# Decay rows of one head side by side in DRAM, so that their loads read runs of 4 KB

## The chip, the cores and the metric

One Trainium2 chip, and of it one core. The metric is the device time of one execution in microseconds (us). The shapes are fixed: one sequence of 1024 tokens with 16 learned meta tokens ahead of it, 1024 channels, 8 heads.

## The reference

One layer of a bidirectional encoder. Each token is normalised and projected once; from the projection come a Fourier branch, and a gated-DeltaNet branch with q, k, v and two sets of decay and beta logits. The delta rule runs forwards and backwards over chunks of 64 tokens. The part of it that the change touches:

```
g = cumsum(g within a chunk of 64)
diff = g[..., :, None] - g[..., None, :]
decay = where(lower, exp(where(lower, diff, 0)), 0)
a_mat = where(strict, (k_beta @ k^T) * decay, 0)
t_mat = inverse(I + a_mat)
qk    = where(lower, (q @ k^T) * decay, 0)
```

So every head, direction and chunk needs a 64 x 64 matrix of exponentials of differences of one row g: one g down the partitions, the same g along the free dimension. After the scan both branches are gated, merged and projected; a mixture of 64 experts (top group, top two experts in it) and a final norm follow.

## The kernel before

The work goes in stages. `norm1` normalises and transposes the input. `gates` computes all decay rows. `heads` makes q, k and v of the 8 heads; `meta` treats the 16 meta tokens. `middle` does the Fourier branch and the gate projections. Then come the scan over chunks (`scan`), the merge (`delta`), the output projection (`output`) and the experts, whose weights stream from DRAM. In `heads` there are 24 tiles (k, v and q of each head, in the order k0 v0 k1 q0 k2 v1 k3 q1 v2 q2 v3 q3, then the same for heads 4 to 7). For each, TensorE does 72 projection matmuls (`product`, L220) into the tile `proj`; ScalarE copies them out (`pad`, L356); VectorE does a convolution of 5 taps (`acc`, eight instructions on L373); ScalarE applies SiLU (`kraw`, `vraw`, `qT`).

For a k tile, `k_stage` transposes (L435), sums squares (L438), takes a reciprocal root in a chain of small VectorE and GpSimd steps (`rk_x` L98, `rk_y` L105, `rk_t` L106 to L108, `rk_y` L109), and scales on ScalarE (`ktok`, L446). `k_back` transposes back on TensorE (L456) to `kT`.

`decay` (L484) builds the 64 x 64 matrices of one head: tile `F`, 128 partitions x 1024 numbers, where a partition is a row in a chunk (two halves of 64), and the free dimension is 16 chunk pairs and directions (`v n`) x 64 columns (`c`). The row along the free dimension must reach all 64 partitions of a half; that is done by a load from the DRAM tensor `dF`, which `gates` wrote (L339). There are two loads for one F (L489), one for each half. Then VectorE subtracts (L494) and limits (L495), and ScalarE exponentiates (L496). `chunks` multiplies F with k k^T (L511, twice, stored to `dL` by L513) or with q k^T (L516, stored to `dQK` by L517). There are 16 such tiles, two for a head; `fp` holds two buffers, so a load of F waits until the store of the F two before it has landed.

`dF` is stored as transposed: its row n is one column of `G` or `FL`, and the 128 columns are ordered `(v n h)`, the head last:

```
L336  self.dF = self.dram("dF", [2, 128, 2, 64])
L339  nc.sync.dma_start(self.dF[i].rearrange("n a c -> n (a c)"), ts[...])
L488  src = self.dF[i].rearrange("(n h) a c -> n h a c", h=8)[:, h, half]
L489  nc.sync.dma_start(F[half]..., src.unsqueeze(0).to_broadcast([64, 16, 64]))
```

`inverse` (L521) gathers `dL` of four heads into `M`, eliminates on VectorE (L688, L690, pairs of growing and shrinking size, ending with the MEMSET on L692) and stores `dT` for the scan.

All loads named here are issued by SyncE (SP), one after the other, and each engine works through its own queue in a fixed order. A scheduler writes these orders when the program is built, from the code and its own estimates; a change in the shape of a transfer therefore moves other instructions too.

Of the kernel before, what the change touches and what calls it, by code (L numbers as in the profile page):

```python
# [8 lines left out]
F32 = mybir.dt.float32  # L9
# [103 lines left out]
class Kern:  # L113
# [116 lines left out]
    def gates(self, abT):  # L230
        tc, nc, io, cp = self.tc, self.nc, self.io, self.c1
# [4 lines left out]
        gp = self.gp  # L236
# [9 lines left out]
        for half in range(2):  # L246
            hs = slice(64 * half, 64 * half + 64)
            for v in range(2):
                d = 0 if half == v else 1
                src = pv[hs, :, 16 * d:16 * d + 16].rearrange("p n (k h) -> p k n h", k=2)  # L250
# [41 lines left out]
        G = cp.tile([128, 136], F32, name="G")  # L292
# [22 lines left out]
        FL = gp.tile([128, 136], F32, name="FL")  # L315
# [11 lines left out]
                    nc.vector.tensor_scalar(FL[hs, cs], G[hs, cs], -1.0, None, op0=OP.mult)  # L327
        self.G, self.PL = G, PL
        tps = self.pprep.tile([128, 512], F32, name="prep")
        nc.tensor.transpose(tps[:, 0:128], G[:, :128], self.ident)  # L330
        nc.tensor.transpose(tps[:, 128:256], FL[:, :128], self.ident)
        nc.tensor.transpose(tps[:8, 256:272], FL[:16, 128:136], self.ident[:16, :16])
        ts = gp.tile([128, 272], F32, name="ts")
        nc.scalar.activation(ts[:, :256], tps[:, :256], AF.Copy)
        nc.scalar.activation(ts[:8, 256:272], tps[:8, 256:272], AF.Copy)
        self.dF = self.dram("dF", [2, 128, 2, 64])  # L336
        self.dFm = self.dram("dFm", [8, 16])
        for i in range(2):
            nc.sync.dma_start(self.dF[i].rearrange("n a c -> n (a c)"), ts[:, 128 * i:128 * i + 128])  # L339
        nc.sync.dma_start(self.dFm, ts[:8, 256:272])  # L340


# [141 lines left out]
    def decay(self, h, d, i):  # L484
        nc = self.nc
        d["F"] = F = self.fp.tile([128, 2, 8, 64], F32, name="F")
        for half in range(2):
            src = self.dF[i].rearrange("(n h) a c -> n h a c", h=8)[:, h, half]  # L488
            nc.sync.dma_start(F[64 * half:64 * half + 64].rearrange("p v n c -> p (v n) c"),  # L489
                              src.unsqueeze(0).to_broadcast([64, 16, 64]))  # L490
        bc = [128, 2, 8, 64]
        c = (self.G, self.PL)[i][:, :128].rearrange("p (v n h) -> p v n h", v=2, h=8)[:, :, :, h:h + 1].to_broadcast(bc)
        m = (self.maskq, self.maskl)[i]
        nc.vector.tensor_tensor(F, *((F, c) if i == 0 else (c, F)), op=OP.subtract)  # L494
        nc.vector.tensor_tensor(F, F, m[:, :, None, :].to_broadcast(bc), op=OP.min)  # L495
        nc.scalar.activation(F, F, AF.Exp)  # L496
# [1284 lines left out]
```

## Time and profile before

| what | value |
|---|---|
| median of 3 runs | 1853.7 us (1852.88 to 1856.15) |
| profiled execution, its time | 1855.85 us |
| profiled execution, its span | 1854.0 us |
| mean granted clock of TensorE | 0.965 |
| TensorE busy | 1726.9 us, 93% of the span |
| VectorE busy | 1043.0 us, 56% |
| ScalarE busy | 696.6 us, 38% |
| GpSimd busy | 194.0 us, 10% |
| DMA packets | 149102, of which 68663 under 512 B |
| heads stage, about | 92 to 464 us |

The span is the profiled execution seen by the profiler; its time is 1.85 us longer, and lies 2.15 us above the median. Busy shares are means over stages with different limits. The stage of the heads is where the slices of the page show TensorE's busy share and its granted clock below full again and again.

### The profile page before, as it was taken

The page shows a single profiled execution, that of the slowest core. Times are in us where ns is not written, and L with a number is a line of the kernel's source. Part 1 is how long each engine was busy: PE and PEld are TensorE (multiplying, and loading weights), DVE is VectorE, ACT ScalarE, POOL GpSimd, SP SyncE. Part 2 cuts the span into 40 slices and gives each one's busy share as a digit, 9 for nine tenths or more (in the row PEclk, how much of TensorE's full clock was granted, in tenths as well). Part 3 has the DMA queues.
Part 4 walks back from the last instruction along what each step waited for, and adds up shares of the span by engine and source line. Part 5 has one row for each costly group of instructions (what it writes and reads, how often), then busy time and mean ns, then how long its engine had stood idle before and what let it go on. Part 6 is the DMA issues. An engine that isn't in the chain of part 4 may idle for free. (4 is left out here: it accounts for less than half of the span.)

```text
span 1854.0 us, 26490 instructions
## 1 busy us (share of the span) xinstructions
PE 1726.9 (93%) x10018; PEld 1237.6 (67%) x10018; DVE 1043.0 (56%) x2196; ACT 696.6 (38%) x1539; POOL 194.0 (10%) x300
## 2 busy tenths in 40 slices
PE   7968989978999999799999999999789999999996
PEld 6968988978978888466766677888634443434342
DVE  6646558777955898456566554641633444434433
ACT  5645546454432211444444443421233332323231
POOL 2000001000010001013323200000110111001100
PEclk9988999988999999899999999999989999999998
DMA  4143542334466346734434327735389999999995
GB/s 156 51 124 114 157 140 93 102 106 132 140 197 177 121 159 205 191 109 137 143 120 120 109 95 239 230 119 204 129 350 419 416 419 419 419 419 415 420 419 202
DMA packets 149102, 391.16 MB, mean 211 GB/s; under 512 B 68663, under 2 KB 70879, under 8 KB 123999
## 3 DMA queue, kind: packets, MB, share of 16 engines
q1 hardware_dynamic: 132744, 337.65, 49.7%
q0 software_dynamic: 14736, 51.02, 8.7%
q8 instruction: 81, 1.33, 0.3%
q10 hardware_dynamic: 1488, 0.73, 0.2%
q14 instruction: 53, 0.43, 0.1%
HBM read 328.28 MB, written 65.26 MB: 212 GB/s over the span
## 5 line engine op out<-in xcount | busy, mean ns | idle before, releaser
L220 PE MATMUL proj<-xh,wh 128*128 128x346 f32 (+5 forms) x1080 | 395.4, 366 | 16.9 <-ACT zt L1696 8.6
L220 PE MATMUL proj<-xl,wh 128*128 128x346 f32 (+4 forms) x1080 | 394.9, 366 | 0.0
L220 PE MATMUL proj<-xh,wl 128*128 128x346 f32 (+4 forms) x1080 | 393.7, 366 | 0.0
L220 PEld LDWEIGHTS proj<-xh,wh 128*128 128x128 f32 (+1 forms) x1080 | 207.8, 192 | 38.1 <-ACT zt L1696 9.4
L220 PEld LDWEIGHTS proj<-xl,wh 128*128 128x128 f32 (+1 forms) x1080 | 207.5, 192 | 18.7 <-issue 5.8
L220 PEld LDWEIGHTS proj<-xh,wl 128*128 128x128 f32 (+1 forms) x1080 | 207.0, 192 | 19.3 <-issue 6.7
L373 DVE SCALAR_TENSOR_TENSOR acc<-pad,convw,acc 128x520 f32<-128x520 f32 x192 | 136.1, 752 | 21.9 <-ACT acc L369 21.8
L860 ACT ACTIVATE wh<-wr 128x1024 fp32r<-128x1024 f32 (+2 forms) x77 | 77.2, 1004 | 130.8 <-PE proj L220 67.6
L861 DVE TENSOR_TENSOR wl<-wr,wh 128x1024 fp32r<-128x1024 f32 (+2 forms) x77 | 88.8, 1155 | 42.6 <-ACT wh L860 42.4
L1343 DVE SCALAR_TENSOR_TENSOR ea<-ea,gw,gu 128x256 f32<-128x256 f32 x32 | 15.4, 480 | 171.7 <-ACT ea L1342 171.7
L688 DVE TENSOR_TENSOR tmp<-M 128x62 f32<-128x62 f32 (+30 forms) x124 | 105.9, 854 | 7.1 <-DMA M<-dL 5.5
L690 DVE TENSOR_TENSOR M<-M,tmp 128x62 f32<-128x62 f32 (+30 forms) x124 | 105.9, 854 | 1.8
L741 DVE SCALAR_TENSOR_TENSOR R<-main,egn,svtok 128x128 f32<-128x128 f32 x128 | 44.8, 350 | 101.5 <-PE main L739 101.4
L750 ACT ACTIVATE vd<-main,vdec 128x128 f32<-128x128 f32 x128 | 46.9, 366 | 137.0 <-PE main L748 136.8
L758 DVE SCALAR_TENSOR_TENSOR S<-S,egl,dS 128x128 f32<-128x128 f32 x240 | 72.7, 343 | 39.6 <-PE dS L757 39.2
L739 PE MATMUL main<-S,skq 128*64 128x128 f32 x1024 | 86.1, 288 | 0.1
L1342 ACT ACTIVATE ea<-gu 128x256 f32<-128x256 f32 x32 | 12.3, 384 | 183.0 <-PE gu L1338 183.0
L1368 DVE TENSOR_TENSOR yl<-dn,yh 128x512 fp32r<-128x512 f32 x64 | 44.2, 690 | 59.9 <-ACT yh L1367 55.0
L739 PEld LDWEIGHTS main<-S,skq 128*64 128x64 f32 x1024 | 54.7, 137 | 31.0 <-DVE so L761 16.5
L1367 ACT ACTIVATE yh<-dn 128x512 fp32r<-128x512 f32 x64 | 38.1, 595 | 97.4 <-PE dn L1365 97.0
L1338 PE MATMUL gu<-ml,gx 128*64 128x512 f32 x288 | 70.8, 607 | 4.1 <-DMA ml<-in_w_gu_dram 4.1
L1338 PE MATMUL gu<-mh,gx 128*64 128x512 f32 x288 | 67.0, 593 | 1.9 <-DMA mh<-in_w_gu_dram 1.9
(432 smaller groups left out, 3160.9 us busy)
## 6 DMA issues: line engine op xcount, KB each, us to landing
mh<-in_w_gu_dram SPq DMA_DIRECT2D x36, 1024.0 KB, 19.9
ml<-in_w_gu_dram SPq DMA_DIRECT2D x36, 1024.0 KB, 21.1
wr<-in_w_t_dram SPq DMA_DIRECT2D x52, 512.0 KB, 4.1
wx<-in_w_gu_dram SPq DMA_DIRECT2D x20, 1024.0 KB, 19.1
mh<-in_w_dn_dram SPq DMA_DIRECT2D x20, 1024.0 KB, 20.9
ml<-in_w_dn_dram SPq DMA_DIRECT2D x18, 1024.0 KB, 19.9
yh<-in_w_gu_dram SPq DMA_DIRECT2D x16, 1024.0 KB, 16.4
yl<-in_w_gu_dram SPq DMA_DIRECT2D x16, 1024.0 KB, 16.5
```

Source lines behind the costliest of these rows:

```text
L220: nc.tensor.matmul(o, w[:, k, :n], x[:, k, a:b], start=(m == 0), stop=(m == 23))
L373: nc.vector.scalar_tensor_tensor(o, pad[:, a + j:a + j + NT // 2], w[:, j:j + 1], o, op0=OP.mult, op1=OP.add)
L688: nc.vector.tensor_tensor(tv, M[:, j + 1:, j:j + 1].to_broadcast([np_, m, j]), M[:, j:j + 1, :j].to_broadcast([np_, m, j]), op=OP.mult)
L690: nc.vector.tensor_tensor(M[:, j + 1:, :j], M[:, j + 1:, :j], tv, op=OP.add)
L739: nc.tensor.matmul(ps[hs[half], i], kv[:, i, 2 * (p % 4) + half], st[half], start=True, stop=True)
L741: nc.vector.scalar_tensor_tensor(R, ps[:, 0], self.egn[:, col:col + 1], d["vtok"][p // 4][:, p % 4], op0=OP.mult, op1=OP.add)
L750: nc.scalar.activation(vd, ps[:, 2], AF.Copy, scale=self.vdec[:, col:col + 1])
L758: nc.vector.scalar_tensor_tensor(st[half], st[half], self.egl[:, half, col:col + 1], dS, op0=OP.mult, op1=OP.add)
L860: self.nc.scalar.activation(hi, src, AF.Copy)
L861: self.nc.vector.tensor_tensor(lo, src, hi.bitcast(F32), op=OP.subtract)
L1338: nc.tensor.matmul(pg[self.HS[i]], d["x"][:, 4 * kk + k, c:c + 64], w[:, 4 * i + k], start=(kk == 0 and k == 0), stop=(kk == 1 and k == 3))
L1368: nc.vector.tensor_tensor(yl[:, cs], pd, yh[:, cs].bitcast(F32), op=OP.subtract)
```

## The change

`gates` reorders the columns of `G` and `FL` from `(n h)` to `(h n)` with two VectorE copies into a new tile `GF`, transposes that instead, and stores `dF` as `[2, 2, 128, 64]`: kind, half, row `(h n)`, column. The store takes four DMAs of 64 columns instead of two of 128. The 16 rows of one head and half are then one run of 16 x 64 x 4 B = 4096 B, and `decay` loads that run to each of 64 partitions instead of 16 pieces of 256 B. Values and consumers are the same.

```diff
         tps = self.pprep.tile([128, 512], F32, name="prep")
-        nc.tensor.transpose(tps[:, 0:128], G[:, :128], self.ident)
-        nc.tensor.transpose(tps[:, 128:256], FL[:, :128], self.ident)
+
+        GF = gp.tile([128, 2, 128], F32, name="GF")
+        for i, t in enumerate((G, FL)):
+            nc.vector.tensor_copy(GF[:, i].rearrange("p (h n) -> p h n", h=8), t[:, :128].rearrange("p (n h) -> p h n", h=8))
+            nc.tensor.transpose(tps[:, 128 * i:128 * i + 128], GF[:, i], self.ident)
...
-        self.dF = self.dram("dF", [2, 128, 2, 64])
+        self.dF = self.dram("dF", [2, 2, 128, 64])
...
         for i in range(2):
-            nc.sync.dma_start(self.dF[i].rearrange("n a c -> n (a c)"), ts[:, 128 * i:128 * i + 128])
+            for a in range(2):
+                nc.sync.dma_start(self.dF[i, a], ts[:, 128 * i + 64 * a:128 * i + 64 * a + 64])
...
         for half in range(2):
-            src = self.dF[i].rearrange("(n h) a c -> n h a c", h=8)[:, h, half]
-            nc.sync.dma_start(F[64 * half:64 * half + 64].rearrange("p v n c -> p (v n) c"),
-                              src.unsqueeze(0).to_broadcast([64, 16, 64]))
+            src = self.dF[i, half, 16 * h:16 * h + 16].rearrange("n c -> (n c)")
+            nc.sync.dma_start(F[64 * half:64 * half + 64].rearrange("p v n c -> p (v n c)"), src.partition_broadcast(64))
```

The order of the instructions moves with it. In the changed kernel the lines of `heads` and after have numbers higher by 4 up to `decay` (L373 becomes L377, the chain of L106 to L109 keeps its numbers), and by 3 from there (L494 becomes L497, L511 becomes L514, L861 becomes L864).

VectorE, between the multiplication that ends the use of the first F (k of head 0) and the subtraction that waits for the load into its buffer (q of head 0), before and after:

```order
L511 SCALAR_TENSOR_TENSOR F<-prep,F 128x512 x2
L495 TENSOR_TENSOR F<-F,cst 128x1024
L373 SCALAR_TENSOR_TENSOR acc<-pad,convw,acc 128x520
L861 TENSOR_TENSOR wl<-wr,wh 128x1024
L373 SCALAR_TENSOR_TENSOR acc<-pad,convw,acc 128x520 x2
L98 TENSOR_SCALAR rk_x<-ssk 128x9
L494 TENSOR_TENSOR F<-F,G 128x1024
```

```order
L514 SCALAR_TENSOR_TENSOR F<-prep,F 128x512 x2
L98 TENSOR_SCALAR rk_x<-ssk 128x9
L497 TENSOR_TENSOR F<-F,G 128x1024
L435 MEMSET ssk 128x1
L377 SCALAR_TENSOR_TENSOR acc<-pad,convw,acc 128x520 x2
```

The subtraction has moved up: of the six instructions that stood between, one is left.

VectorE, the root chain of head 0 (`rk_x` to `rk_y`) and the first subtraction (k of head 0), before and after:

```order
L98 TENSOR_SCALAR rk_x<-ssk 128x9
L431 MEMSET ssk 128x1
L106 TENSOR_TENSOR rk_t<-rk_y 128x9
L107 TENSOR_TENSOR rk_t<-rk_t,rk_x 128x9
L108 TENSOR_SCALAR rk_t<-rk_t 128x9
L109 TENSOR_TENSOR rk_y<-rk_y,rk_t 128x9
L447 TENSOR_SCALAR km<-prep,rk_y 16x128
L861 TENSOR_TENSOR wl<-wr,wh 128x1024
L373 SCALAR_TENSOR_TENSOR acc<-pad,convw,acc 128x520 x3
L494 TENSOR_TENSOR F<-PL,F 128x1024
```

```order
L106 TENSOR_TENSOR rk_t<-rk_y 128x9
L377 SCALAR_TENSOR_TENSOR acc<-pad,convw,acc 128x520
L497 TENSOR_TENSOR F<-PL,F 128x1024
L377 SCALAR_TENSOR_TENSOR acc<-pad,convw,acc 128x520
L107 TENSOR_TENSOR rk_t<-rk_t,rk_x 128x9
L497 TENSOR_TENSOR F<-PL,F 128x1024
L498 TENSOR_TENSOR F<-F,cst 128x1024
L108 TENSOR_SCALAR rk_t<-rk_t 128x9
L498 TENSOR_TENSOR F<-F,cst 128x1024
L864 TENSOR_TENSOR wl<-wr,wh 128x1024
L109 TENSOR_TENSOR rk_y<-rk_y,rk_t 128x9
```

The chain of head 0 stood ahead of every F; now the first two subtractions stand inside it.

SP, from the store of k of head 1 (`dL`) to the loads of F for heads 2 and 3, before and after:

```order
L513 DMA dL<-F 64x2x512 x2
L517 DMA dQK<-F 128x1024
L489 DMA F<-dF 64x16x64 x4
L448 DMA dk<-ktok 128x1024
L199 DMA wr<-in_w_t_dram 128x1024
```

```order
L516 DMA dL<-F 64x2x512 x2
L493 DMA F<-dF 64x1024 x2
L520 DMA dQK<-F 128x1024
L493 DMA F<-dF 64x1024 x2
L521 DMA dkq<-qT 128x1024
```

The first of the two loads no longer stands behind the store of q of head 0.

## Rows read from the trace of the kernel before

**Rows 1.** The page, its first line and busy time of TensorE: us, share of the span, instructions.

```profile
span 1854.0 us, 26490 instructions
```

**Rows 2.** Busy time in four stretches (us from the span's start): length, then busy us and instructions of PE, PEld, DVE, ACT and POOL, then the granted clock of TensorE, the DMA share and GB/s.

```profile
92.00:278.00 186.00, 152.25 (x1133) 148.00 (x1131) 103.26 (x159) 93.02 (x198) 7.59 (x23) 0.90 0.44 133
278.00:464.00 186.00, 163.93 (x1145) 158.61 (x1146) 141.78 (x198) 94.02 (x221) 12.25 (x22) 0.91 0.34 108
464.00:740.00 276.00, 274.48 (x1435) 229.14 (x1434) 209.66 (x302) 73.20 (x108) 13.32 (x22) 1.00 0.52 166
...
1340.00:1854.00 514.00, 482.56 (x2186) 202.14 (x2186) 210.35 (x425) 159.27 (x297) 51.39 (x53) 0.97 0.95 391
```

**Rows 3.** The waits of PE between 92 and 464 us, the longest entry: who waited <- for whom: us in total, times, longest us.

```profile
PE prep L456 <- ACT ktok L446: 32.4, 7, 9.2
```

**Rows 4.** The view of the tile F: who waited for its loads (us, times), and the time of its DMAs from issue to landing.

```profile
  DVE F L494: 91.7, 16
...
DMA to landing us min/median/max: 3.2/11.1/14.4
```

**Rows 5.** Timeline of DVE, the 16 subtractions on L494 in order: start us, us, engine, instruction, and in brackets the idle time before it and what ended it.

```profile
102.36 1.23 DVE L494 TENSOR_TENSOR F<-PL,F 128x1024 f32<-128x1024 f32 x1 [7.61 <-DMA F<-dF]
...
108.30 1.23 DVE L494 TENSOR_TENSOR F<-PL,F 128x1024 f32<-128x1024 f32 x1 [2.24 <-DMA F<-dF]
...
129.52 1.23 DVE L494 TENSOR_TENSOR F<-F,G 128x1024 f32<-128x1024 f32 x1 [8.19 <-DMA F<-dF]
...
168.76 1.23 DVE L494 TENSOR_TENSOR F<-PL,F 128x1024 f32<-128x1024 f32 x1 [11.05 <-DMA F<-dF]
173.74 1.23 DVE L494 TENSOR_TENSOR F<-PL,F 128x1024 f32<-128x1024 f32 x1 [1.83 <-DMA F<-dF]
...
201.45 1.22 DVE L494 TENSOR_TENSOR F<-F,G 128x1024 f32<-128x1024 f32 x1 [5.07 <-issue]
...
244.79 1.23 DVE L494 TENSOR_TENSOR F<-F,G 128x1024 f32<-128x1024 f32 x1 [1.97 <-DMA F<-dF]
253.28 1.23 DVE L494 TENSOR_TENSOR F<-F,G 128x1024 f32<-128x1024 f32 x1 [3.55 <-DMA F<-dF]
273.68 1.22 DVE L494 TENSOR_TENSOR F<-PL,F 128x1024 f32<-128x1024 f32 x1 [8.15 <-issue]
...
290.09 1.23 DVE L494 TENSOR_TENSOR F<-PL,F 128x1024 f32<-128x1024 f32 x1 [8.04 <-DMA F<-dF]
332.29 1.22 DVE L494 TENSOR_TENSOR F<-F,G 128x1024 f32<-128x1024 f32 x1 [7.62 <-DMA F<-dF]
...
373.87 1.23 DVE L494 TENSOR_TENSOR F<-PL,F 128x1024 f32<-128x1024 f32 x1 [8.66 <-issue]
...
388.17 1.22 DVE L494 TENSOR_TENSOR F<-PL,F 128x1024 f32<-128x1024 f32 x1 [6.58 <-DMA F<-dF]
422.62 1.23 DVE L494 TENSOR_TENSOR F<-F,G 128x1024 f32<-128x1024 f32 x1 [6.36 <-DMA F<-dF]
...
461.93 1.23 DVE L494 TENSOR_TENSOR F<-F,G 128x1024 f32<-128x1024 f32 x1 [3.67 <-issue]
468.05 1.23 DVE L494 TENSOR_TENSOR F<-F,G 128x1024 f32<-128x1024 f32 x1 [1.13 <-DMA F<-dF]
```

**Rows 6.** Timelines of DVE, ACT and PE between 129 and 140 us, behind the third of these waits: the last step of the root chain, the scaling of k, and the transpose that waits for it.

```profile
137.33 0.17 DVE L109 TENSOR_TENSOR rk_y<-rk_y,rk_t 128x9 f32<-128x9 f32 x1
...
139.33 2.17 ACT L446 ACTIVATE ktok<-prep,rk_y 128x128 f32<-128x128 f32 x8
...
139.74 0.48 PE L456 MATMUL prep<-cst,ktok 128*128 128x128 f32 x1 [9.16 <-ACT ktok L446]
```

**Rows 7.** The stretch from 92 to 464 us in 186 windows of 2 us, columns as in rows 2: the first and the last window with a granted clock below 1.00.

```profile
102.00:104.00 2.00, 0.00 (x0) 0.00 (x0) 1.64 (x2) 1.28 (x1) 0.00 (x0) 0.99 0.44 110
...
444.00:446.00 2.00, 2.00 (x27) 1.88 (x24) 2.00 (x2) 1.07 (x3) 0.00 (x0) 0.68 0.45 97
```

**Rows 8.** DMA issues over the whole span: engine, count, KB each, median us from issue to landing. `wr` is a load of a projection weight, 128 partitions x 4096 B.

```profile
wr<-in_w_t_dram SPq DMA_DIRECT2D x52, 512.0 KB, 4.1
...
F<-dF SPq DMA_DIRECT2D x32, 256.0 KB, 11.7
...
dL<-F SPq DMA_DIRECT2D x16, 256.0 KB, 3.2
```

**Rows 9.** Timeline of SP: start us, us that the issues took, and how many.

```profile
87.78 0.81 SPq L339 DMA_DIRECT2D dF<-ts  x2
...
112.10 1.25 SPq L513 DMA_DIRECT2D dL<-F  x2
116.02 1.31 SPq L489 DMA_DIRECT2D F<-dF  x2
```

**Rows 10.** Timeline of DVE: a step over 128 x 128 numbers in `gates`, two taps of the convolution, and the split of a weight.

```profile
81.01 0.22 DVE L305 TENSOR_SCALAR egn<-eg 128x128 f32<-128x128 f32 x1
...
109.45 1.43 DVE L373 SCALAR_TENSOR_TENSOR acc<-pad,convw,acc 128x520 f32<-128x520 f32 x2
...
113.79 1.22 DVE L861 TENSOR_TENSOR wl<-wr,wh 128x1024 fp32r<-128x1024 f32 x1
```

**Rows 11.** The end of the first inverse on DVE (timeline), and the Fourier matmuls of PE (view of line 613: count, duration ns min/median/max, first and last start us).

```profile
531.31 0.11 DVE L692 MEMSET M<- 128x64 f32 x1
...
L613 PE MATMUL four<-tab,AB x240: 272/282/388, 565.9 to 624.9; 128*128 128x260 f32 x100, 9*128 9x260 f32 x20
```

## Prediction

> **What bounds the kernel now.** I read the span first: 1854.0 us [rows 1]. The profiled execution took 1855.85 us, which is 2.15 us above the median of the runs shown (1853.7); the sum below is made against 1855.85, and 2.15 us come off at the end.
>
> Then the busy time by stretch. The reader should see in [rows 2] that TensorE is the busy engine nearly everywhere (274.48 of 276 us from 464 to 740 us, clock 1.00), that the experts' stage after 1340 us has the DMA engines busy at a share of 0.95, and that the heads, 92 to 464 us, are the exception: TensorE idles 33.75 us in the first half and 22.07 us in the second, 55.8 us together, at a granted clock of 0.90 and 0.91. In 2-us windows, its busy time multiplied by what the clock lacks to 1.00 sums to 24.4 us; 47 of the 186 windows lie below 1.00, the first and last of them are in [rows 7]. So this stage holds 55.8 + 24.4 = 80.2 us that TensorE could give back.
>
> Then who makes it wait. The largest entry of TensorE's waits is the transpose on L456 behind ScalarE's `ktok`, 32.4 us [rows 3]. Nothing of F stands in that row. But VectorE works in order, and the view of F says that the subtraction on L494 waited 91.7 us in 16 times [rows 4], one for every F. One stall shows the link: VectorE waits 8.19 us for a load until 129.52 [rows 5]; the rest of the root chain stands behind that subtraction and ends at 137.33; ScalarE scales at 139.33; TensorE, idle 9.16 us, starts at 139.74 [rows 6]. The other long waits in [rows 5] have such a stall beside them too. So I take it that 91.7 us of VectorE's waits cost TensorE the 80.2 us: 0.875 us for one.
>
> **The change part by part.**
>
> *The loads.* One F is two loads of 256 KB, each 64 partitions x 16 pieces of 256 B; they land 11.1 us after issue in the middle [rows 4]. A projection weight is 512 KB as 128 rows of 4096 B and lands in 4.1 us [rows 8]. After the change a pair of F loads is as many bytes in as many pieces as one weight. No row shows one 4-KB source read by 64 partitions, so the price has two ends: 3.2 us, the store of one half of F [rows 8], and 11.1 us, as now, if the pieces were not what costs. I take 4.1 us, by the row with the same pieces and the same direction, plus 0.4 us because the second load is issued later: 4.5 us in place of 11.1, so 6.6 us earlier for every F.
>
> *The order.* The scheduler has put work closer together too, so less VectorE work covers each load. I counted the instructions between the one that frees a buffer and the subtraction that waits for the load into it, at 0.71 us for one of the eight convolution instructions of a tile, 1.22 us for a weight split [rows 10], 1.22 us for a step on F [rows 5], and a step of the elimination as the row of its size. For q of head 0 it is 4.7 us before (1.22 + 3 x 0.71 + 1.22 + 0.17) and 0.2 us now: 4.5 us less. For the 14 loads that reuse a buffer, in order, the cover falls by 4.5, 1.8, 2.1, 2.1, -1.0, -0.4, 1.7, 0.7, -0.9, 2.2, 3.0, 1.5, 4.3 and 4.0 us (a minus is a gain). Each wait in [rows 5] then becomes the wait, less 6.6, plus that number, and not below 0. The first two loads reuse nothing: 7.61 - 6.6 = 1.0, and 0. The others give 6.1, 6.25, 0, 0.6, 0, 0, 3.25, 2.1, 0.1, 4.3, 3.0, 1.3, 1.4, 0. Sum 29.4 us in place of 91.7: VectorE waits 62.3 us less, and TensorE gets 62.3 x 0.875 = 54.5 us. What is late next in the stage is the same subtraction, at q of head 0 (6.1) and k of head 2 (6.25), since the store of the older F still has to land first: 112.10 to 116.02 [rows 9].
>
> *What is added.* Two copies of 128 x 128 stand ahead of the transposes in `gates`; the row of that size is 0.22 us [rows 10], and a step on eight times the numbers, 1.22 us [rows 5], bounds a slow stride. I take 0.22 each. Two more stores of `dF` cost SP 0.42 us each, half of 0.81 [rows 9]. All of it is ahead of the first F: 1.3 us, with 3.3 us as the upper end (two slow copies) and 0 as the lower, since VectorE waits for the first F anyway. The Trainium skill, DMA: Bandwidth & Descriptors, Specifications, asks for at least 512 B in a transfer and says that smaller ones are done as read-modify-write, which speaks against these stores: their runs fall from 512 to 256 B. No row here prices that alone; if it doubled the 2 us from the first store to the first load, 2 us would go from the sum.
>
> *The weight loads, `dk` and `dkq`* behind the loads of F on SP gain by the same packets; I cost this at nothing, since no wait on them is left in the stage that does not lie behind F as well.
>
> *After the heads.* A gain counts only if it reaches the end. From 464 to 740 us TensorE is full, and VectorE has 66 us free [rows 2]. The Fourier matmuls start at 565.9, after the first inverse has ended on VectorE at 531.31 [rows 11]. In the new order 297 projection matmuls stand between the last chunk products of the heads and the first Fourier step, 294 before, and the inverse has as many steps left at that point, so the stages keep their distance and move together. The expert weights are fetched when the output stage is done, so the stream after 1340 us moves as well.
>
> **Sum.** 1855.85 - 54.5 + 1.3 = 1802.65 us for an execution like the profiled one; less 2.15, **1800.5 us** against the median.
>
> **The rivals.**
>
> *All of it comes back.* The lesser cover is partly a fiction: TensorE runs faster too, and VectorE waits for convolution inputs at other places, which covers loads that my count leaves bare. Then 80.2 - 1.3 = 78.9 us come off: 1774.8. For it: every long stall lies behind an F. Against it: the bare place at q of head 0, and VectorE, busy 141.78 of 186 us in the second half [rows 2], with TensorE's need only a little above that.
>
> *The two halves go one after the other.* Then the pair lands after 2 x 3.2 = 6.4 us, 4.7 us earlier than now. The waits sum to 51 us, VectorE gains 41, TensorE 36, less 1.3: 1819. Against it: the two stores of `dL`, of the same size, were issued from 112.10 and had both landed by 116.02, 3.9 us [rows 9]. The Trainium skill, DMA: Bandwidth & Descriptors, Rules for kernel authors, says that transfers to disjoint halves of the partitions serialise, because both use all 16 engines. By that rule it would be this case; the row of 3.9 us for two halves does not agree.
>
> *VectorE becomes the bound in the second half.* There the elimination of the first inverse fills its gaps. If what it no longer waits for F it waits elsewhere, only the first half gains: the first nine waits of [rows 5] sum to 49.7 us, and 17.2 of them would be left, so 32.5 x 0.875 - 1.3 = 27 us come off: 1827.
>
> *Slower: the landing stays.* If 64 reads of one place in DRAM, and not the count of pieces, set the 11.1 us, or if the load is still cut into small pieces, so that the change does not do what it says, only the lesser cover is left. With nothing earlier the 16 waits sum to 117 us, 26 more than now: 22.5 us for TensorE, and 1.3: 1877.5. It decides from a landing of about 9.4 us upwards; below that the change gains. Against it: 512 KB in 4-KB rows land in 4.1 us [rows 8].
>
> **How the numbers follow.** Forecast (1788 to 1814) 0.48; all of it 0.17; halves in turn 0.16; VectorE bound 0.09; slower 0.07; and 0.03 for nothing that can be measured, where the new order gives back what the loads bring. A measurement of this kernel can tell about 0.2% from no change, 3.7 us. Faster is the sum of the first four, 0.90; same 0.03; slower 0.07. The range leaves out the slower case, no change, and the outer half of "all of it": 1775 to 1832. The likeliest case alone is 1788 to 1814.
>
> **What would show it.** Right: F loads landing in 4 to 5 us; the waits of L497 near 30 us instead of 91.7; TensorE's idle time between 92 and the end of the heads near 20 us and its clock there near 0.96; the first inverse ending and the Fourier matmuls starting some 53 us earlier; the same time from there to the end. The longest waits left should be at q of head 0 and k of head 2. Wrong: a landing above 6 us; waits of VectorE or TensorE of the same sum under another name (`acc` behind ScalarE, `pad` behind TensorE); or an earlier end of the heads with a new gap of TensorE before the Fourier matmuls or at the first step of the scan.

## The result and the profile after

The changed kernel takes 1783.17 us (median of 4 runs, 1780.85 to 1787.33), the kernel before, run beside it, 1853.29 us: a ratio of 0.9622, 95% interval [0.96, 0.9643]. That is 70.1 us less. The forecast was 1800.5 us in a range of 1775 to 1832: the direction and the stage were right, the gain was 17 us larger, so that the time fell just below the 1788 to 1814 us of the likeliest case, and one reason given for it turned out wrong (below).

The first line of the page, which answers to [rows 1], then the busy time by stretch of the kernel after, two of the stretches of [rows 2] (length, busy us and instructions of PE, PEld, DVE, ACT and POOL, granted clock, DMA share, GB/s):

```profile
span 1782.4 us, 26489 instructions
```

```profile
92.00:278.00 186.00, 181.74 (x1388) 177.29 (x1387) 136.95 (x216) 117.00 (x260) 12.61 (x31) 0.98 0.51 153
278.00:464.00 186.00, 183.18 (x1298) 174.84 (x1296) 171.65 (x253) 93.55 (x199) 9.15 (x16) 0.98 0.43 136
```

TensorE idles 4.26 and 2.82 us where it idled 33.75 and 22.07, and its clock is 0.98 where it was 0.90 and 0.91. Summed over 2-us windows, what the clock lacks costs 6.8 us instead of 24.4. So of the 80.2 us that TensorE lost between 92 and 464 us, 13.9 are left: 66.3 came back. From the start of the heads to 860 us, where both kernels are inside the scan, the same sums give 98.8 us before and 30.3 after, 68.5 less.

The loads of F, on their own line, in the kernel after (who waited for them: us, times; and their time to landing). [Rows 4] showed 91.7 us in 16 waits, and [rows 8] 11.7 us for the load:

```profile
  DVE F L497: 19.2, 12
...
DMA to landing us min/median/max: 3.4/4.3/6.7
```

The two longest waits that are left, on VectorE, with what ran just ahead of them; [rows 5] holds the ones before (start us, us, instruction, in brackets the idle time before it):

```profile
122.98 0.17 DVE L98 TENSOR_SCALAR rk_x<-ssk 128x9 f32<-128x9 f32 x1 [7.46 <-ACT sqk L446]
125.42 1.23 DVE L497 TENSOR_TENSOR F<-F,G 128x1024 f32<-128x1024 f32 x1 [2.26 <-DMA F<-dF]
...
153.40 0.17 DVE L98 TENSOR_SCALAR rk_x<-ssk 128x9 f32<-128x9 f32 x1
156.73 1.23 DVE L497 TENSOR_TENSOR F<-PL,F 128x1024 f32<-128x1024 f32 x1 [3.17 <-DMA F<-dF]
```

These are q of head 0 and k of head 2, the two places that the forecast had named, with 2.26 and 3.17 us instead of its 6.1 and 6.25. And TensorE's wait for `ktok`, 32.4 us in 7 times in [rows 3]:

```profile
PE prep L460 <- ACT ktok L450: 2.2, 3, 1.4
```

SyncE's issues at the start of the heads, where the first loads follow the stores of `dF`:

```profile
90.12 1.75 SPq L343 DMA_DIRECT2D dF<-ts  x4
91.92 0.38 SPq L344 DMA_DIRECT2D dFm<-ts  x1
92.58 2.42 SPq L493 DMA_DIRECT2D F<-dF  x4
```

The stores start 2.34 us later than the 87.78 of [rows 9] and take 0.94 us longer, so the first load goes out 2.7 us later than before; its subtraction starts at 97.66 us instead of 102.36 all the same, behind a wait of 1.50 us where it was 7.61:

```profile
97.66 1.23 DVE L497 TENSOR_TENSOR F<-PL,F 128x1024 f32<-128x1024 f32 x1 [1.50 <-DMA F<-dF]
```

The gain is kept to the end. The first inverse ends at 462.9 us instead of 531.3 and the Fourier matmuls start at 497.1 instead of 565.9 [rows 11], 68.4 and 68.8 us earlier; the scan starts 69.9 us earlier, and the span is 71.6 us shorter.

### The profile page after: what moved, and what is told of

Same layout as the page of the kernel before. It is cut to its first block, busy times and chain, and to the rows that moved or that the text cites. A ratio compares the mean times of both kernels' runs of the same rounds, so it can differ in the third digit from the quotient of the medians.

```text
span 1782.4 us, 26489 instructions
## 1 busy us (share of the span) xinstructions
PE 1709.2 (96%) x10018; PEld 1222.1 (69%) x10018; DVE 1043.3 (59%) x2198; ACT 693.9 (39%) x1537; POOL 195.0 (11%) x300
## 5 line engine op out<-in xcount | busy, mean ns | idle before, releaser
L220 PE MATMUL proj<-xh,wh 128*128 128x346 f32 (+5 forms) x1080 | 389.9, 361 | 8.3 <-ACT zt L1699 6.0
L220 PE MATMUL proj<-xl,wh 128*128 128x346 f32 (+4 forms) x1080 | 390.4, 362 | 0.0
L220 PE MATMUL proj<-xh,wl 128*128 128x346 f32 (+4 forms) x1080 | 389.2, 361 | 0.0
L220 PEld LDWEIGHTS proj<-xh,wh 128*128 128x128 f32 (+1 forms) x1080 | 203.7, 189 | 28.2 <-ACT zt L1699 6.4
L220 PEld LDWEIGHTS proj<-xl,wh 128*128 128x128 f32 (+1 forms) x1080 | 203.7, 189 | 18.7 <-issue 5.8
L220 PEld LDWEIGHTS proj<-xh,wl 128*128 128x128 f32 (+1 forms) x1080 | 203.2, 188 | 19.1 <-issue 6.6
L377 DVE SCALAR_TENSOR_TENSOR acc<-pad,convw,acc 128x520 f32<-128x520 f32 x192 | 135.5, 753 | 17.0 <-ACT acc L373 16.9
L864 DVE TENSOR_TENSOR wl<-wr,wh 128x1024 fp32r<-128x1024 f32 (+2 forms) x77 | 88.9, 1156 | 50.5 <-ACT wh L863 42.5
## 6 DMA issues: line engine op xcount, KB each, us to landing
yh<-in_w_gu_dram SPq DMA_DIRECT2D x16, 1024.0 KB, 19.8
```

The source lines that it names most:

```text
L220: nc.tensor.matmul(o, w[:, k, :n], x[:, k, a:b], start=(m == 0), stop=(m == 23))
L377: nc.vector.scalar_tensor_tensor(o, pad[:, a + j:a + j + NT // 2], w[:, j:j + 1], o, op0=OP.mult, op1=OP.add)
L864: self.nc.vector.tensor_tensor(lo, src, hi.bitcast(F32), op=OP.subtract)
```

## The experiments

All times are medians of runs with the kernel before beside them, each of the three sets on a chip of its own (before: 1852.7 us beside e1 to e4, 1851.5 beside e5 to e8, 1853.06 beside e9 to e12). The landing is the median of the loads of F on their own line; the profile has it for only some of the 32 loads: 5 in the kernel before, 22 after, 25 in e6, and 6 to 10 in e1 to e4 and e9 to e12. The waits of VectorE for F count all 16 tiles.

**Does the number of pieces set the landing?** That was the reason given in the forecast. e1 keeps the new layout but gives each row of `dF` 80 numbers of room, so that the 16 rows of a head can't be read as one run: 16 pieces of 256 B again, as before, 320 B apart.

```diff
-        self.dF = self.dram("dF", [2, 2, 128, 64])
+        self.dF = self.dram("dF", [2, 2, 128, 80])
...
-            src = self.dF[i, half, 16 * h:16 * h + 16].rearrange("n c -> (n c)")
+            src = self.dF[i, half, 16 * h:16 * h + 16, :64]
```

> The rows of one head and half lie near each other in DRAM as in the changed kernel, but at a pitch of 320 B, so that each load is again 16 pieces of 256 B to a partition. Theory 1 (the number of pieces sets the landing, and the landing sets the time): F lands in about 11 us, VectorE waits 80 to 110 us for it, 1840 to 1875 us. Rival 2 (what counts is that the rows of a head are close together, not how many pieces they come in): landing under 6 us, 1775 to 1800 us. Rival 3 (the gain is that of the new order of instructions, not of the landing): 1775 to 1800 us even with a late landing.

e2, e3 and e4 put 2, 4 and 8 of the 64-number rows together with room for one more behind them, so that a load has 8 pieces of 512 B, 4 of 1 KB or 2 of 2 KB for a partition. For e3:

```diff
+        self.dF = self.dram("dF", [2, 2, 32, 320])
...
+            src = self.dF[i, half, 4 * h:4 * h + 4, :256]
```

> Pieces of 512 B: 8 to a partition, by a gap after every second row. This kernel and the ones with pieces of 1 KB and 2 KB have the same instructions in the same order on every engine; only the pieces differ. Theory 1, with the landing in proportion to the pieces between 256 B (11.1 us) and 4 KB (4.2 us): 7.4 us, VectorE waits about 60 us for F, about 1815 to 1825 us. Rival 3 (order): no difference over 4 us among the three. Rival 4 (only pieces under 512 B are slow): landing 4 to 5 us, 1780 to 1790 us, as with 1 KB and 2 KB.

> Pieces of 1 KB, the same order of instructions as with 512 B and 2 KB. Theory 1: landing 5.6 us, waits for F about 38 us, about 1795 to 1805 us. Rival 3 (order): the same time as with 512 B within 4 us. Rival 4 (only under 512 B is slow): 1780 to 1790 us.

> Pieces of 2 KB, the same order of instructions as with 512 B and 1 KB. Theory 1: landing 4.7 us, waits for F about 26 us, about 1785 to 1793 us. Rival 3 (order): the same time as with 512 B within 4 us. Rival 4: 1780 to 1790 us.

| kernel | pieces of a load | landing, us | F waits of VectorE, us | time, us | ratio to before |
|---|---|---|---|---|---|
| before | 16 x 256 B | 11.7 | 91.7 | 1853.3 | |
| e1 | 16 x 256 B | 4.8 | 10.2 | 1791.69 | 0.9668 [0.9645, 0.9691] |
| e2 | 8 x 512 B | 4.5 | 19.8 | 1785.14 | 0.9626 |
| e3 | 4 x 1 KB | 4.5 | 19.2 | 1784.05 | 0.9629 |
| e4 | 2 x 2 KB | 4.1 | 17.4 | 1780.42 | 0.9603 |
| after | 1 x 4 KB | 4.3 | 19.2 | 1783.17 | 0.9622 [0.96, 0.9643] |

The loads of F in e1:

```profile
  DVE F L498: 10.2, 6
...
DMA to landing us min/median/max: 3.8/4.8/7.8
```

So as many pieces of the same size as before, and a landing of 4.8 us. The page says that the pieces are there: 149390 DMA packets, before 149102, after 118670. The theory of the pieces falls. From 256 B to 4 KB the landing moves by 0.5 us. The Trainium skill, DMA: Bandwidth & Descriptors, Specifications, asks for 512 B and more in a transfer; that limit can't be seen in these loads (4.8 us in pieces of 256 B, 4.5 in pieces of 512 B).

**Is there more to win from the loads?** e5 leaves the loads of F out and subtracts from the mask instead.

```diff
-        for half in range(2):
-            src = ...
-            nc.sync.dma_start(F[64 * half:64 * half + 64]..., src.partition_broadcast(64))
...
+        L = m[:, :, None, :].to_broadcast(bc)
+        nc.vector.tensor_tensor(F, *((L, c) if i == 0 else (c, L)), op=OP.subtract)
```

> The changed kernel without the loads of F: the subtraction reads the mask in place of the loaded row (so the decay matrices are not those of the reference). It shows what is left to gain from the loads. Theory 1 at TensorE's share found for the change (72.5 us less waiting of VectorE for 71.6 us of span): the 19.2 us that VectorE still waits bring at most 13.9 us, what TensorE still loses in the heads by idling and by its clock, so 1769 to 1776 us. Rival 5 (VectorE is already the bound of the second half): 1780 to 1786 us.

It takes 1789.23 us, 0.9657 of before: not faster than the change. TensorE still loses 5.7 us to idling and 3.4 to the clock between 92 and 464 us (after: 7.1 and 6.8), and 16.4 and 9.6 us between 464 and 740 us (after: 10.2 and 5.1). The scan starts at 689.9 us, after the change at 684.1. So 9.1 of the 13.9 us that are left in the stage of the heads are there without any load of F, and the 4.8 us that it saves there are outweighed by some 11 us more between 464 and 740. The order of the instructions differs between the two kernels as well, and its part wasn't separated. e1 shows the same: VectorE waits 9 us less for F than in the change, and the kernel is 8.5 us slower.

**Would more buffers have done it?** A load of F waits until its buffer is free. e6 is the kernel before with four buffers in `fp` instead of two, e7 the changed one with four, e8 the changed one with three.

```diff
-self.fp = c3.enter_context(tc.tile_pool(name="fp", bufs=2))
+self.fp = c3.enter_context(tc.tile_pool(name="fp", bufs=4))
```

> The kernel before, loads of 256-B pieces as they were, but four buffers for F instead of two, so that a load need not wait for the store of the F two before. Theory 1 (it is the lateness of the landing that costs, so issuing earlier does as well): VectorE waits 20 to 45 us for F instead of 91.7, 1795 to 1825 us. Rival 6 (the 32768 small pieces cost by keeping the DMA queues and SP busy, whenever they are issued, and delay the other loads and stores): 1835 us or more.

> The changed kernel with four buffers for F. Theory 1: the waits left for F fall from 19.2 us to under 6 us, since the round trip of store and load no longer counts; up to 13 us off, 1771 to 1779 us. Rival 5 (VectorE is already the bound): 1780 to 1786 us.

> The changed kernel with three buffers for F. Theory 1: most of the same, waits for F under 10 us, 1772 to 1780 us. Rival 5: 1780 to 1786 us.

e6 is 1.4% slower than before, 1877.28 us, ratio 1.0137 [1.0118, 1.0156]: theory 1's 1795 to 1825 us missed, and the rival's 1835 us or more came true. Its loads on line 489:

```profile
  DVE F L494: 92.2, 16
...
DMA to landing us min/median/max: 7.4/10.1/16.3
```

The waits stay, and the landing stays late (10.1 us, 11.7 before). But more buffers did not put the loads earlier either: in its own queue SyncE still waits for stores of F before it issues loads of F, 45.7 us from 92 to 420 us in these two rows (38.5 us in the kernel before):

```profile
SPq L489 <- DMA dQK<-F: 27.7, 4, 9.0
SPq L489 <- DMA dL<-F: 18.0, 5, 7.4
```

From the issue of a pair's second load to the moment when VectorE is ready for it, the median is 4.4 us; in the kernel before it is 5.0. So e6 doesn't tell whether an earlier issue would have hidden the late landing. With these waits TensorE loses 60.7 + 32.7 us from 92 to 464 us (before 55.8 + 24.4), and 15.9 + 2.7 from 464 to 740 (before 1.5 + 0). How much of that the new order of the instructions causes, and how much the transfers, wasn't separated. e7 takes 1787.57 us (0.9657), e8 1781.03 (0.9627), with F waits of 21.7 and 16.8 us where theory 1 expected under 6 and under 10: buffers bring nothing here.

**What sets the landing, then?** In the kernel before, the rows of one head stand 8 rows of 512 B apart, so the 16 pieces of a load lie exactly 4096 B apart in DRAM. In e1 to e4 and after the change no two do. Theory 2 says that this distance costs the 7 us. e9 is the kernel before with rows of 576 B, pieces 4608 B apart, and nothing else (the store writes the same 512 B of each row): every engine's instructions keep the order of before.

```diff
-        self.dF = self.dram("dF", [2, 128, 2, 64])
+        self.dF = self.dram("dF", [2, 128, 144])
...
-            src = self.dF[i].rearrange("(n h) a c -> n h a c", h=8)[:, h, half]
+            src = self.dF[i, :, 64 * half:64 * half + 64].rearrange("(n h) c -> n h c", h=8)[:, h]
```

> The kernel before, its instructions in its own order on every engine, with one difference: a row of dF takes 576 B of DRAM instead of 512, so that the 16 pieces that one load of F gathers stand 4608 B apart instead of 4096 B. The pieces stay 16 of 256 B for a partition. Theory 2 (the distance of exactly 4096 B between the pieces sets the 11.1 us): landing about 4 us, the waits of VectorE for F shrink from 91.7 to about 10 us (each of the 16 less 7.1, not below 0), the time falls by 82 x 0.875 = 72 us to about 1780. Rival, closeness (pieces that are kilobytes apart are slow, whatever the distance): landing 11 us, 1852, no change. Rival, the order of the instructions gave the gain: even with a landing of 4 us the time stays above 1835.

It takes 1777.93 us (1773.55 to 1784.83), ratio 0.9603 [0.9577, 0.9629]: all of the gain, with the old order, the old loop and the old pieces. Its loads on line 489, and the busy time by stretch:

```profile
  DVE F L494: 8.5, 4
...
DMA to landing us min/median/max: 3.8/5.2/7.6
```

```profile
92.00:278.00 186.00, 185.40 (x1429) 182.24 (x1428) 143.63 (x222) 121.60 (x278) 14.19 (x31) 0.99 0.63 164
278.00:464.00 186.00, 184.99 (x1313) 175.04 (x1312) 166.84 (x245) 94.22 (x180) 7.80 (x16) 0.99 0.46 134
```

The expectation had been 1780 us, from each wait in [rows 5] less 7.1 us and 0.875 us of TensorE for one of VectorE. The waits fell by 83.2 us and the time by 75.1, 0.90 for one.

e10, e11 and e12 go the other way: e1 with the pieces 4096, 4352 and 2048 B apart, in e1's order on every engine. The edit of e10 (1088 numbers in e11, 512 in e12):

```diff
-        self.dF = self.dram("dF", [2, 2, 128, 80])
+        self.dF = self.dram("dF", [2, 2, 128, 1024])
```

> The kernel e1 (the new layout with padded rows, 16 pieces of 256 B for a partition) in the same order on every engine, with a row of dF taking 4096 B instead of 320 B: the 16 pieces of a load stand 4096 B apart, as in the kernel before. Theory 2 (the distance of 4096 B): landing back at about 11 us, the waits for F from 10.2 to between 92 and 124 us, the time up by 82 to 114 x 0.875, to 1860 to 1890. Rival, the order gave the gain: about 1792, as e1, whatever the landing. Rival, the landing was set by something else in the old layout (rows of 512 B shared by the two halves): landing 4 us, 1792.

> As e10, in the same order, with 4352 B from piece to piece instead of 4096. Theory 2 in its exact form (a multiple of 4096 B): landing 4 us, F waits about 10 us, 1792. Rival, closeness (anything kilobytes apart): landing about 11 us, 1860 to 1890, as e10.

> As e10, in the same order, with 2048 B from piece to piece. If only a distance of 4096 B or its multiples counts piece by piece: landing 4 us and 1792. If pieces at the same place within 4096 B get in each other's way, there are two such places here in place of one, each with half of the pieces: a landing between 4 and 11 us, about 6 to 8, F waits 30 to 60, 1810 to 1835. Closeness: as e11.

| kernel | from piece to piece | landing, us | F waits, us | time, us | ratio to before |
|---|---|---|---|---|---|
| e1 | 320 B | 4.8 | 10.2 | 1791.69 | 0.9668 [0.9645, 0.9691] |
| e11 | 4352 B | 5.1 | 11.1 | 1797.17 | 0.9691 [0.9673, 0.971] |
| e12 | 2048 B | 6.9 | 27.9 | 1806.87 | 0.9743 [0.9725, 0.9761] |
| e10 | 4096 B | 9.8 | 73.9 | 1859.54 | 1.0034 [1.0017, 1.0051] |

The loads on line 493 of e10 (pieces 4096 B apart):

```profile
  DVE F L498: 73.9, 15
...
DMA to landing us min/median/max: 6.9/9.8/10.8
```

of e11 (4352 B):

```profile
  DVE F L498: 11.1, 7
...
DMA to landing us min/median/max: 3.9/5.1/6.3
```

and of e12 (2048 B):

```profile
  DVE F L498: 27.9, 9
...
DMA to landing us min/median/max: 4.1/6.9/8.7
```

256 B more or less between the pieces is worth 62.4 us of the kernel (e10 against e11). That pieces lie kilobytes apart does no harm (e11, e9), so closeness falls as a reason. Half the distance, 2048 B, lies between, as if pieces at the same place within 4096 B got in each other's way: 16 at one place in e10, 8 at each of two in e12. Counted so, e9 has 2 at each of eight (4608 is 4096 + 512) and lands in 5.2 us, and e11 has 1 at each and lands in 5.1. e12 landed in the 6 to 8 us forecast for that and came out just below the forecast in the rest (27.9 us of waits where 30 to 60 were expected, 1806.9 us where 1810 was the lower end), and e10's landing and waits came out below the 11 and the 92 to 124 us expected, its time (1859.5) just under the lower end of 1860. The size of `dF` is not the reason: it is about 2 MB in both e10 and e11. Which part of the memory the pieces share isn't shown; a distance of 1024 B, and 4096 B with fewer pieces, were not tried.

The order of the instructions gave no gain by itself: e9 has all of it in the order of before, and e10, in the order of e1 but with the old distance, is 0.3% slower than before. (The order of the change itself was not run with the old distance.)

## Why the prediction was right, and where not

- **The bound.** Right. The stage held 80.2 us of TensorE's idle time and missing clock; 66.3 came back when F's loads came sooner, although no row of TensorE names F; in e9, where nothing but the distance of the pieces changed, it was 75.2. The link was VectorE's order: `ktok` fell from 32.4 to 2.2 us with the waits for F.
- **The landing.** The figure was right, 4.1 us for a load and 4.5 for the pair against 4.3 and some 4.9 measured; its reason was wrong. It was taken from a weight load with as many 4-KB pieces [rows 8], as if the count of pieces had cost the 11 us. e1 has the count of before and lands in 4.8 us, e10 has the same count and size, only moved to 4096 B, and lands in 9.8. The weight row and the new load agree because neither has what makes the old one slow; the change removed the many pieces and their distance of 4096 B at once, so that a wrong reason gave the right figure, which was luck. Whether the 64 partitions that read the same places add to the late landing, as the rival "the landing stays" had it, was not tried: all loads of F have them. The row that the forecast lacked was one for many small pieces at another distance.
- **The halves in turn.** Did not happen: a load lands in 4.3 us in the middle and its partner is issued about 0.6 us later, so a pair is there after some 4.9 us; in turn it would be 6.4.
- **The order and the lesser cover.** Too dear: 29.4 us of waits were expected and 19.2 are there, 10.2 x 0.875 = 8.9 us of the 17. Most of it is a misread row. The 11.1 us that the forecast took for the loads is the middle of all transfers of the tile F, its stores among them [rows 4]; the loads alone took 11.7 [rows 8]. From 11.7 to 4.3 us a load lands 7.4 us earlier and not 6.6, and with 7.4 the forecast's own sum of the 16 waits gives 21.4 us. The cover was counted well: VectorE's work between the two instructions fell by 4.69 us at q of head 0, where the forecast had 4.5. The places were right, their size not: at q of head 0 the subtraction waits 2.26 us, not 6.1, because VectorE has just waited 7.46 us for ScalarE at `rk_x`, and that wait covers the load too. The rival "all of it comes back" said as much, for the inputs of the convolution: a cover counted in instructions leaves out the waits between them. The result, 1783.2, lies between the two, 1774.8 and 1800.5.
- **The rate.** 72.5 us of waits less brought 70.1 us, 0.97 for one instead of 0.875: 6.7 us of the 17. In the stage itself it is 66.3 / 72.5 = 0.91; e9 gave 0.90. That the ratio is not the same all over shows at the small end: below some 20 us of waits the time no longer follows them (e1 10.2 us and 1791.7, after 19.2 and 1783.2, in different orders). In the one order of e1 and e10, 63.7 us more of waits cost 67.9 us, 1.07 for one.
- **What is added.** 1.3 us was expected, and the first load does go out 2.7 us later, within the bounds of 0 to 3.3. VectorE still waits 1.50 us for that load, but TensorE is busy 19.63 of the 20 us from 92 to 112 us at a clock of 1.00, so the delay cost it next to nothing; that is the last 1.3 of the 17. The two copies took 0.27 and 0.28 us. From the first store to the first load it is 2.46 us, 2.08 before; it did not double.
- **Slower, because the landing stays.** The condition named there, a late landing in a new order, was nearly met on purpose in e10: landing 9.8 us, 1859.5, 0.3% slower than before. Neither the point from which it decides, 9.4 us, nor its price, 1877.5 at 11.1 us, can be tested against that run, since its order is not that of the change, and both were worked out from the misread 11.1.
- **After the heads.** Right: inverse, Fourier matmuls and scan move by 68 to 70 us together, and the expert stage by 71.9 (from 1361.4 to 1289.5 us).

## What to carry over

A gather (one load of many pieces that lie apart) that lands late for its bytes may be suffering from the distance of its pieces, not from their size: look at the stride in bytes before the layout is rebuilt, and try a pad first. Here 64 B more in a row of `dF`, and nothing else, does as much as the new layout (0.9603 [0.9577, 0.9629] against 0.9622 [0.96, 0.9643]). And when a transfer's price is taken from another row, ask which of the things in which the two differ the row can speak for, and whether its figure is of the loads alone; here size, count and place had all changed together, and one pair of runs with a single number altered told them apart.

## What the runs showed of the hardware

- Loads of 64 partitions x 16 pieces of 256 B landed in 9.8 us (e10), 10.1 (e6) and 11.7 (before) with 4096 B from piece to piece, in 6.9 with 2048 B, and in 4.8 to 5.2 with 320, 4352 or 4608 B. The Trainium skill, DMA: Bandwidth & Descriptors, Latency and other measured facts, reports a loss for copies whose rows lie 2 MiB or more apart, cured by a pad of 4 KiB but not by 192 B, and calls sharing of memory channels an inference. Here a distance of 4 KB is enough, and a pad of 256 B cures it; no run shows whether it is the same mechanism.
- The issue is held up too: SyncE took 9.03 us over its first four loads of F in the kernel before, and 3.54 in e9, which issues the same four with as many pieces (7.50 in e10 and 3.76 in e11, which differ in the distance alone):

```profile
89.86 9.03 SPq L489 DMA_DIRECT2D F<-dF  x4
```

```profile
89.61 3.54 SPq L489 DMA_DIRECT2D F<-dF  x4
```

- In these loads 256-B pieces cost next to nothing at a good distance: 4.8 us for 16 of them 320 B apart, 4.3 for one piece of 4 KB.
